# Attention in a two-layer hybrid trunk: row maximum negated, and exponentials issued, per pair of heads

## The chip, the cores and the metric

The kernel runs on one core of a Trainium2 chip. The core's engines work side by side, each through its own queue in order, and meet at semaphores: TensorE (PE: matrix products and transposes; PEld is its loading of stationary operands), VectorE (DVE), ScalarE (ACT), GpSimd (POOL), and SyncE (SP), which here only issues DMAs. The metric is the device time of one execution in microseconds; the value shown is a median of runs.

## The reference

Two layers of a decoder trunk over 512 tokens of width 1024 in float32. Each layer normalises x, projects it to 6400 columns, runs two groups of heads side by side (a gated linear recurrence, HGRN2, and sliding-window attention with a learned sink per head), gates both, projects back and adds. The attention has 16 query heads of 64 and 2 key/value heads. The part that the change touches is the softmax with sink over a window of 128 keys:

```python
def sliding_window_attention(q, k, v, sinks):
    ...
    s = jnp.einsum('bnqkgd,bnskd->bnkgqs', qb, kw).astype(jnp.float32) * ATT_SCALE
    ...
    band = (diff >= 0) & (diff < WINDOW)
    ...
    s = jnp.where(mask[None, :, None, None, :, :], s, NEG_INF)
    sink = jnp.broadcast_to(sinks.astype(jnp.float32).reshape(KV, G)[None, None, :, :, None, None],
                            s.shape[:-1] + (1,))
    p = jax.nn.softmax(jnp.concatenate([s, sink], axis=-1), axis=-1)[..., :-1]
    o = jnp.einsum('bnkgqs,bnskd->bnqkgd', p.astype(v.dtype), vw)

def hybrid_layer(x, w_in, w_out, g_pre, g_post, lb, g_head, sinks):
    h = rms_norm(x, g_pre)
    proj = jnp.einsum('bsd,de->bse', h, w_in)
    ...
    y = jnp.einsum('bse,ed->bsd', jnp.concatenate([o_h, o_a], axis=-1), w_out)
    return x + rms_norm(y, g_post)
```

## The kernel before

**Projections.** Float32 products are made of three products each: every operand is split into a rounded part and a rest (`hi`, `lo`), and `mm3` (L174 to L177) issues lo x hi, hi x lo and hi x hi. Weights come in pieces of 128x512 (`raw`, a DMA on SP), ACT casts each (`whi`, L169) and DVE, for one slab POOL, subtracts (`wlo`, L170); nine pairs of buffers hold them. A slab is eight pieces, 512 columns of the projection. `step()` issues one `mm3` and keeps loading and casting a few pieces ahead.

**Attention.** Layer by layer, `run()` (L769) merges the attention stream with the projection steps of the following slabs (inputs and forget gates): of two streams, the one that is least far on comes next. So PE always has projection products between the attention's small ones. The stream goes through 16 units (g, n): g is a group of four heads, n a block of 128 queries. At its i-th turn it issues `att_scores` of unit i, `att_transpose` of unit i-2 and `att_value` of unit i-4.

- `att_scores` (L406): PE computes the scores of four heads. For n = 0 (units 0, 4, 8, 12) there is one block of keys, and four heads fit one bank of PSUM: DVE masks (copy_predicated L420) and takes the max (L421). For the other twelve units each head has two blocks of keys, so two banks are used, two heads in each, which I call the first and the second half: on each half DVE puts the valid score of the two blocks in one place (copy_predicated L432, by the mask of the window) and takes the max (L433). Then, for all four heads, DVE makes `negm` (the smaller of the negated scaled max and the negated sink, L436) and `ds` (sink plus negm, L438), and ACT makes four exponentials from PSUM to `s` with their row sums (L442) and the exponential of `ds` (L445). DVE adds and inverts the sums (L446, L447), and POOL multiplies `s` with the result (L449).
- `att_transpose` (L452): four transposes on PE into a bank (L455), which ACT casts (`a`, L267) and DVE subtracts (`lo`, named `a` too, L268); for n > 0 POOL then selects the parts that belong to the current and the previous block of keys (`pcur` or `b`, and `pprev`, L467).
- `att_value` (L474): products with v on PE (L481), a copy on ACT (`u`, L483), an addition on DVE (`oa`, L487).

**Banks.** Three PSUM banks, `sc_78` to `sc_80` in the trace's longer names, go round among the halves of scores and the transposes (and later the recurrence). A new use waits for the last reader of the use before: for scores these are the exponentials, for transposes the `lo` subtraction.

**What sets the order.** The program's order is a wish; a scheduler sets each engine's queue from it by a model of times. Matrix products wrapped in `pin` (`tc.keep_in_program_order`) keep their order among each other. The operations on DVE, ACT and POOL are free to move where their data allow.

Of the kernel before, what the change touches and what calls it, by code (L numbers as in the profile page):

```python
# [10 lines left out]
F32 = mybir.dt.float32  # L11
# [54 lines left out]
def hybrid_kernel(ctx: ExitStack, tc: tile.TileContext, x, wkv, win, wout, g_pre, g_post, lbp, ghead, sinks,  # L66
# [28 lines left out]
    def tmp(tag, dt=F32, n=1):  # L95

        t = tp.tile([P, n, 512] if n > 1 else [P, 512], dt, tag=tag, name=tag, bufs=TB[tag])
        return t
# [225 lines left out]
    def layer(l, last):  # L324
# [81 lines left out]
        def att_scores(g, n):  # L406
            v = g // 2
            q = qs[g]
            hs = slice(4 * g, 4 * g + 4)
            t_ = slice(n * P, (n + 1) * P)  # L410
            mx_ = sm.tile([P, 4], F32, tag="mx", name="mx")
            cur = []
            if n == 0:
                S = sc()
                for h in range(4):
                    for p in range(2):
                        pin(nc.tensor.matmul(S[:, h * P:(h + 1) * P], lhsT=q[:, h, t_], rhs=kst[v][p][:, 0:P],
                                         start=(h == 0 and p == 0), stop=(h == 3 and p == 1)))
                Sv = S.rearrange("p (h s) -> p h s", h=4)
                nc.vector.copy_predicated(Sv, am4, neg.unsqueeze(2).broadcast_to([P, 4, P]))  # L420
                nc.vector.tensor_reduce(mx_, Sv, axis=AX.X, op=ALU.max)  # L421
                cur = [Sv[:, h, :] for h in range(4)]
            else:
                for hp_ in range(2):
                    S = sc()
                    for h in range(2):
                        for p in range(2):
                            pin(nc.tensor.matmul(S[:, h * 256:(h + 1) * 256], lhsT=q[:, 2 * hp_ + h, t_],  # L428
                                             rhs=kst[v][p][:, (n - 1) * P:(n + 1) * P],
                                             start=(h == 0 and p == 0), stop=(h == 1 and p == 1)))  # L430
                    Sv = S.rearrange("p (h s) -> p h s", h=2)
                    nc.vector.copy_predicated(Sv[:, :, P:2 * P], am2, Sv[:, :, 0:P])  # L432
                    nc.vector.tensor_reduce(mx_[:, 2 * hp_:2 * hp_ + 2], Sv[:, :, P:2 * P], axis=AX.X, op=ALU.max)  # L433
                    cur += [Sv[:, h, P:2 * P] for h in range(2)]
            negm = sm.tile([P, 4], F32, tag="negm", name="negm")
            nc.vector.scalar_tensor_tensor(negm, mx_, -SCALE, nsnk[:, l, hs], op0=ALU.mult, op1=ALU.min)  # L436
            ds_ = sm.tile([P, 4], F32, tag="ds", name="ds")
            nc.vector.tensor_tensor(ds_, snk[:, l, hs], negm, op=ALU.add)  # L438
            pt = tmp("s")
            sums = sm.tile([P, 4], F32, tag="sums", name="sums")  # L440
            for h in range(4):
                nc.scalar.activation(pt[:, h * P:(h + 1) * P], cur[h], AF.Exp, bias=negm[:, h:h + 1], scale=SCALE,  # L442
                                     accum_out=sums[:, h:h + 1])
            es = sm.tile([P, 4], F32, tag="es", name="es")
            nc.scalar.activation(es, ds_, AF.Exp)  # L445
            nc.vector.tensor_tensor(sums, sums, es, op=ALU.add)  # L446
            nc.vector.reciprocal(sums, sums)  # L447
            pv = pt.rearrange("p (h s) -> p h s", h=4)
            nc.gpsimd.tensor_tensor(pv, pv, sums.unsqueeze(2).broadcast_to([P, 4, P]), op=ALU.mult)  # L449
            return pt  # L450
# [458 lines left out]
```

## Time and profile before

| | us |
|---|---|
| median of three runs | 962.07 (960.97 to 962.83) |
| the profiled execution, its own time | 959.31 |
| its span, first to last instruction | 957.6 |
| PE busy in the span | 921.2 (96%) |
| DVE busy | 683.7 (71%) |
| ACT busy | 478.4 (50%) |
| POOL busy | 268.9 (28%) |
| mean granted clock of PE | 0.986 |
| attention of layer 0, of layer 1 | about 79 to 186, 551 to 658 from the span's start |

The engines overlap, so busy times don't add up to the span. A wait counts for the time only where PE waits, or where something waits for it that PE waits for. In a timeline a row is one instruction or several of a kind in a row, with its start, its time, and in brackets the idle time of the engine ahead of it and what ended that by the profile. The granted clock is that of PE as a share of full speed.

### The profile page before, as it was taken

The page shows a single profiled execution, that of the slowest core. Times are in us where ns is not written, and L with a number is a line of the kernel's source. Part 1 is how long each engine was busy: PE and PEld are TensorE (multiplying, and loading weights), DVE is VectorE, ACT ScalarE, POOL GpSimd, SP SyncE. Part 2 cuts the span into 40 slices and gives each one's busy share as a digit, 9 for nine tenths or more (in the row PEclk, how much of TensorE's full clock was granted, in tenths as well). Part 3 has the DMA queues.
Part 4 walks back from the last instruction along what each step waited for, and adds up shares of the span by engine and source line. Part 5 has one row for each costly group of instructions (what it writes and reads, how often), then busy time and mean ns, then how long its engine had stood idle before and what let it go on. Part 6 is the DMA issues. An engine that isn't in the chain of part 4 may idle for free.

```text
span 957.6 us, 19092 instructions
## 1 busy us (share of the span) xinstructions
PE 921.2 (96%) x7228; PEld 757.5 (79%) x7228; DVE 683.7 (71%) x1382; ACT 478.4 (50%) x1135; POOL 268.9 (28%) x282
## 2 busy tenths in 40 slices
PE   7999999999999999999979998999999999999996
PEld 5888777777878888788868886877788887887885
DVE  5766888786757785765794678878867568849546
ACT  5434656836545462334552365676374545514242
POOL 2322454422231221211231234434322213113102
PEclk9999999999999999999989999999999999999998
DMA  6366433122413343324452775112223123513313
GB/s 227 101 197 201 137 81 89 52 71 67 122 46 89 90 132 89 107 71 112 133 163 66 198 209 155 34 56 88 79 58 98 55 79 100 155 51 107 88 45 132
DMA packets 56716, 101.34 MB, mean 106 GB/s; under 512 B 6448, under 2 KB 8880, under 8 KB 56624
## 3 DMA queue, kind: packets, MB, share of 16 engines
q1 hardware_dynamic: 56624, 100.12, 35.1%
q8 instruction: 57, 0.93, 0.4%
q14 instruction: 35, 0.29, 0.1%
HBM read 87.52 MB, written 12.58 MB: 105 GB/s over the span
## 4 chain that ended last, share of the span: by engine, by line
PE 78%; DVE 11%; ACT 6%; issue 2%; POOL 2%; DMA 1%; SPq 0%; DVEq 0%; POOLq 0%; ACTq 0%
PE pj L175 22%; PE pj L177 22%; PE pj L176 21%; DVE wlo L170 3%; PE sc L583 2%; PE sc L428 2%; PE ac L652 1%; ACT s L442 1%; PE ac L655 1%; PE ac L640 1%; DVE oa L487 1%; PE ac L481 1%; DVE q L600 1%; PE sc L455 1%; PE sc L700 1%
## 5 line engine op out<-in xcount | busy, mean ns | idle before, releaser
L169 ACT CAST whi<-raw 128x512 fp32r<-128x512 f32 x256 | 157.2, 621 | 131.2 <-PE pj L177 61.0
L170 DVE TENSOR_TENSOR wlo<-raw,whi 128x512 fp32r<-128x512 f32 x248 | 190.1, 778 | 44.8 <-ACT whi L169 42.4
L175 PE MATMUL pj<-hhi,wlo 128*128 128x512 f32 x512 | 206.0, 402 | 0.0
L177 PE MATMUL pj<-hhi,whi 128*128 128x512 f32 x512 | 200.1, 391 | 0.0
L176 PE MATMUL pj<-hlo,whi 128*128 128x512 f32 x512 | 199.5, 390 | 0.0
L177 PEld LDWEIGHTS pj<-hhi,whi 128*128 128x128 f32 x512 | 96.1, 188 | 21.0
L175 PEld LDWEIGHTS pj<-hhi,wlo 128*128 128x128 f32 x512 | 96.2, 188 | 18.6
L176 PEld LDWEIGHTS pj<-hlo,whi 128*128 128x128 f32 x512 | 96.3, 188 | 18.0
L175 PE MATMUL pj<-whi,ops 128*128 128x512 f32 x256 | 103.8, 406 | 0.0
L175 PE MATMUL pj<-whi,hlo 128*128 128x512 f32 x256 | 103.0, 405 | 0.0
L176 PE MATMUL pj<-wlo,hhi 128*128 128x512 f32 x256 | 102.1, 399 | 0.0
L177 PE MATMUL pj<-whi,hhi 128*128 128x512 f32 x256 | 101.4, 396 | 0.0
L177 PE MATMUL pj<-whi,ops 128*128 128x512 f32 x256 | 100.1, 391 | 0.0
L176 PE MATMUL pj<-wlo,ops 128*128 128x512 f32 x256 | 99.7, 390 | 0.0
L601 POOL TENSOR_TENSOR k<-k,tot 128x256 f32<-128x256 f32 x80 | 66.0, 844 | 109.5 <-PE sc L583 60.5
L600 DVE TENSOR_TENSOR q<-q,tot 128x256 f32<-128x256 f32 x80 | 48.3, 629 | 14.5 <-PE sc L594 7.6
L442 ACT ACTIVATE s<-sc,negm 128x128 f32<-128x128 f32 x128 | 45.6, 370 | 25.7 <-DVE negm L436 25.4
L449 POOL TENSOR_TENSOR s<-s,sums 128x512 f32<-128x512 f32 x32 | 34.4, 1074 | 83.4 <-DVE sums L447 47.9
L177 PEld LDWEIGHTS pj<-whi,hhi 128*128 128x128 f32 x256 | 48.9, 191 | 10.2
L177 PEld LDWEIGHTS pj<-whi,ops 128*128 128x128 f32 x256 | 48.0, 188 | 10.7
L176 PEld LDWEIGHTS pj<-wlo,hhi 128*128 128x128 f32 x256 | 49.2, 192 | 8.4
L175 PEld LDWEIGHTS pj<-whi,hlo 128*128 128x128 f32 x256 | 48.8, 191 | 8.6
(172 smaller groups left out, 1594.8 us busy)
## 6 DMA issues: line engine op xcount, KB each, us to landing
raw<-in_win_dram SPq DMA_DIRECT2D x192, 256.0 KB, 2.7
raw<-in_wout_dram SPq DMA_DIRECT2D x64, 256.0 KB, 2.7
stack<-rot SPq DMA_DIRECT2D x16, 512.0 KB, 4.4
qs<-stack SPq DMA_DIRECT2D x32, 256.0 KB, 5.0
a<-in_x_dram SPq DMA_DIRECT2D x12, 256.0 KB, 2.9
raw<-in_wkv_dram SPq DMA_DIRECT2D x8, 256.0 KB, 4.0
x_mid<-a SPq DMA_DIRECT2D x8, 256.0 KB, 2.1
a<-x_mid SPq DMA_DIRECT2D x8, 256.0 KB, 2.9
```

Source lines behind the costliest of these rows:

```text
L169: nc.scalar.copy(hi, v)
L170: (nc.gpsimd if i in on_pool and i % 2 else nc.vector).tensor_tensor(lo, v, hi.bitcast(F32), op=ALU.subtract)
L175: nc.tensor.matmul(o, lhsT=sta[1], rhs=mov[0], start=start, stop=False)
L176: nc.tensor.matmul(o, lhsT=sta[0], rhs=mov[1], start=False, stop=False)
L177: nc.tensor.matmul(o, lhsT=sta[0], rhs=mov[0], start=False, stop=stop)
L428: pin(nc.tensor.matmul(S[:, h * 256:(h + 1) * 256], lhsT=q[:, 2 * hp_ + h, t_], rhs=kst[v][p][:, (n - 1) * P:(n + 1) * P], start=(h == 0 a ...
L442: nc.scalar.activation(pt[:, h * P:(h + 1) * P], cur[h], AF.Exp, bias=negm[:, h:h + 1], scale=SCALE, accum_out=sums[:, h:h + 1])
L449: nc.gpsimd.tensor_tensor(pv, pv, sums.unsqueeze(2).broadcast_to([P, 4, P]), op=ALU.mult)
L455: pin(nc.tensor.transpose(T[:, h * P:(h + 1) * P], pt[:, h * P:(h + 1) * P], ident))
L583: pin(nc.tensor.matmul(L[32 * b:32 * b + 32, c:c + 16], lhsT=k[:, o_:o_ + 32], rhs=qv[:, blk:blk + qu, 1, :], start=True, stop=True, tile_ ...
L600: nc.vector.tensor_tensor(qv[:, :, 1, :], qv[:, :, 1, :], tv[:, :, 0].unsqueeze(2).broadcast_to([P, nb, hh]), op=ALU.mult)
L601: nc.gpsimd.tensor_tensor(kv_[:, :, 0, :], kv_[:, :, 0, :], tv[:, :, 1].unsqueeze(2).broadcast_to([P, nb, hh]), op=ALU.mult)
```

## The change

In `att_scores` the buffers are taken at the top, and a helper `exps` makes negm for the heads it is given, two columns or four, and at once their exponentials. It is called after each half's max, no longer once after both. `pin` on the second half's copy_predicated keeps the order of such operations among pinned ones on DVE. `ds` and all that follows stay for four heads at a time. There are 24 more negm operations, 12 in each layer; no other operation is added or taken away. The lines of the changed kernel differ: negm is L417, the exponentials L420, copy_predicated L430 and L442, max L431 and L445, `ds` L447, `es` L449, sums L450 and L451, the multiply L453; from there on each line is 4 higher.

```diff
@@ -408,8 +408,18 @@
             q = qs[g]
             hs = slice(4 * g, 4 * g + 4)
             t_ = slice(n * P, (n + 1) * P)
-            mx_ = sm.tile([P, 4], F32, tag="mx", name="mx")
-            cur = []
+            mx_, negm, ds_, sums = (sm.tile([P, 4], F32, tag=n_, name=n_) for n_ in ("mx", "negm", "ds", "sums"))
+            pt = tmp("s")
+
+            def exps(first, cur):
+
+                c = slice(first, first + len(cur))
+                nc.vector.scalar_tensor_tensor(negm[:, c], mx_[:, c], -SCALE, nsnk[:, l, 4 * g + first:4 * g + first + len(cur)],
+                                               op0=ALU.mult, op1=ALU.min)
+                for h, src in enumerate(cur, first):
+                    nc.scalar.activation(pt[:, h * P:(h + 1) * P], src, AF.Exp, bias=negm[:, h:h + 1], scale=SCALE,
+                                         accum_out=sums[:, h:h + 1])
+
             if n == 0:
                 S = sc()
                 for h in range(4):
@@ -419,7 +429,7 @@
                 Sv = S.rearrange("p (h s) -> p h s", h=4)
                 nc.vector.copy_predicated(Sv, am4, neg.unsqueeze(2).broadcast_to([P, 4, P]))
                 nc.vector.tensor_reduce(mx_, Sv, axis=AX.X, op=ALU.max)
-                cur = [Sv[:, h, :] for h in range(4)]
+                exps(0, [Sv[:, h, :] for h in range(4)])
             else:
                 for hp_ in range(2):
                     S = sc()
@@ -429,18 +439,12 @@
                                              rhs=kst[v][p][:, (n - 1) * P:(n + 1) * P],
                                              start=(h == 0 and p == 0), stop=(h == 1 and p == 1)))
                     Sv = S.rearrange("p (h s) -> p h s", h=2)
-                    nc.vector.copy_predicated(Sv[:, :, P:2 * P], am2, Sv[:, :, 0:P])
+                    cp = nc.vector.copy_predicated(Sv[:, :, P:2 * P], am2, Sv[:, :, 0:P])
+                    if hp_:
+                        pin(cp)
                     nc.vector.tensor_reduce(mx_[:, 2 * hp_:2 * hp_ + 2], Sv[:, :, P:2 * P], axis=AX.X, op=ALU.max)
-                    cur += [Sv[:, h, P:2 * P] for h in range(2)]
-            negm = sm.tile([P, 4], F32, tag="negm", name="negm")
-            nc.vector.scalar_tensor_tensor(negm, mx_, -SCALE, nsnk[:, l, hs], op0=ALU.mult, op1=ALU.min)
-            ds_ = sm.tile([P, 4], F32, tag="ds", name="ds")
+                    exps(2 * hp_, [Sv[:, h, P:2 * P] for h in range(2)])
             nc.vector.tensor_tensor(ds_, snk[:, l, hs], negm, op=ALU.add)
-            pt = tmp("s")
-            sums = sm.tile([P, 4], F32, tag="sums", name="sums")
-            for h in range(4):
-                nc.scalar.activation(pt[:, h * P:(h + 1) * P], cur[h], AF.Exp, bias=negm[:, h:h + 1], scale=SCALE,
-                                     accum_out=sums[:, h:h + 1])
             es = sm.tile([P, 4], F32, tag="es", name="es")
             nc.scalar.activation(es, ds_, AF.Exp)
             nc.vector.tensor_tensor(sums, sums, es, op=ALU.add)
```

The scheduler makes another order of it on all engines, within the attention stages only, and the same in both layers. Three places follow, all in layer 0: unit 7 on DVE and on ACT, units 2 to 5 on PE, and the stage's start on POOL.

On DVE, from unit 7's first half on, before:

```order
L432 COPY_PREDICATED sc_78<-masks,sc_78 128x2x128
L446 TENSOR_TENSOR sums<-sums,es 128x4
L433 TENSOR_REDUCE mx<-sc_78 128x2
L447 RECIPROCAL sums<-sums 128x4
L432 COPY_PREDICATED sc_79<-masks,sc_79 128x2x128
L268 TENSOR_TENSOR a<-sc_80,a 128x512
L170 TENSOR_TENSOR wlo<-raw,whi 128x512 x3
L433 TENSOR_REDUCE mx<-sc_79 128x2
L487 TENSOR_TENSOR oa<-ac,u 64x2x128
L436 SCALAR_TENSOR_TENSOR negm<-mx,nsnk 128x4
L487 TENSOR_TENSOR oa<-ac,u 64x2x128
L438 TENSOR_TENSOR ds<-snk,negm 128x4
```

The same place in the changed kernel:

```order
L442 COPY_PREDICATED sc_78<-masks,sc_78 128x2x128
L445 TENSOR_REDUCE mx<-sc_78 128x2
L450 TENSOR_TENSOR sums<-sums,es 128x4
L417 SCALAR_TENSOR_TENSOR negm<-mx,nsnk 128x2
L451 RECIPROCAL sums<-sums 128x4
L170 TENSOR_TENSOR wlo<-raw,whi 128x512
L442 COPY_PREDICATED sc_79<-masks,sc_79 128x2x128
L170 TENSOR_TENSOR wlo<-raw,whi 128x512
L445 TENSOR_REDUCE mx<-sc_79 128x2
L417 SCALAR_TENSOR_TENSOR negm<-mx,nsnk 128x2
L447 TENSOR_TENSOR ds<-snk,negm 128x4
L268 TENSOR_TENSOR a<-sc_80,a 128x512
```

Unit 7's first max is now followed by a negm of two columns, ahead of the weight subtractions (`wlo`) that lay between the first copy and the second half's max; one `wlo` stands between the two halves' small steps, and two others have moved.

On ACT around unit 7's exponentials, before:

```order
L169 CAST whi<-raw 128x512 x2
L483 COPY u<-ac 64x512
L169 CAST whi<-raw 128x512
L442 ACTIVATE s,sums<-sc_78,negm 128x128 x2
L442 ACTIVATE s,sums<-sc_79,negm 128x128 x2
L445 ACTIVATE es<-ds 128x4
```

In the changed kernel (exponentials L420):

```order
L420 ACTIVATE s,sums<-sc_78,negm 128x128
L169 CAST whi<-raw 128x512
L420 ACTIVATE s,sums<-sc_78,negm 128x128
L516 COPY vt<-pj 128x512
L267 CAST a<-sc_80 128x512
L420 ACTIVATE s,sums<-sc_79,negm 128x128 x2
L449 ACTIVATE es<-ds 128x4
```

The two halves' exponentials stand further apart, with a weight cast, a copy and a cast of transposes between them.

On PE, from the transposes of unit 2 (the first row's `sc_80`) to those of unit 3, before:

```order
L455 MATMUL sc_80<-ident,s 128x128 x4
L481 MATMUL ac<-pcur,vst 128x512 x2
L481 MATMUL ac<-pprev,vst 128x512 x2
L175 MATMUL pj<-whi,hlo 128x512
L176 MATMUL pj<-wlo,hhi 128x512
L177 MATMUL pj<-whi,hhi 128x512
L175 MATMUL pj<-whi,hlo 128x512
L455 MATMUL sc_80<-ident,s 128x128 x4
```

In the changed kernel, where the transposes of unit 2 stand two rows ahead of this piece, and the row between is one product L177:

```order
L438 MATMUL sc_78<-kst,qs 128x256 x4
L176 MATMUL pj<-wlo,hhi 128x512
L177 MATMUL pj<-whi,hhi 128x512
L175 MATMUL pj<-whi,hlo 128x512
L176 MATMUL pj<-wlo,hhi 128x512
L177 MATMUL pj<-whi,hhi 128x512
L485 MATMUL ac<-pcur,vst 128x512 x2
L485 MATMUL ac<-pprev,vst 128x512 x2
L175 MATMUL pj<-whi,hlo 128x512
L176 MATMUL pj<-wlo,hhi 128x512
L459 MATMUL sc_80<-ident,s 128x128 x4
```

The first half of unit 5's scores (into `sc_78`) has moved behind the transposes of unit 2, and more products stand between the transposes of unit 2 and of unit 3, whose bank is the same.

On POOL, the first operations of the attention stage, before (L449 is the multiply of a unit's exponentials, L467 the two selections):

```order
L449 TENSOR_TENSOR s<-s,sums 128x512 x3
L467 AFFINE_SELECT pcur<-a 128x1024
L467 AFFINE_SELECT pprev<-a 128x1024
L449 TENSOR_TENSOR s<-s,sums 128x512
L467 AFFINE_SELECT b<-a 128x1024
L467 AFFINE_SELECT pprev<-a 128x1024
L449 TENSOR_TENSOR s<-s,sums 128x512
L467 AFFINE_SELECT pcur<-a 128x1024
```

In the changed kernel, where these are L453 and L471:

```order
L453 TENSOR_TENSOR s<-s,sums 128x512 x4
L471 AFFINE_SELECT pcur<-a 128x1024
L471 AFFINE_SELECT pprev<-a 128x1024
L471 AFFINE_SELECT b<-a 128x1024
L471 AFFINE_SELECT pprev<-a 128x1024
L471 AFFINE_SELECT pcur<-a 128x1024
L453 TENSOR_TENSOR s<-s,sums 128x512
L471 AFFINE_SELECT pprev<-a 128x1024
```

Four multiplies now stand ahead of the first selections, and a selection of unit 3 ahead of the multiply of unit 4.

## Rows read from the trace of the kernel before

**Rows 1.** The page's first part: busy time, share of the span, instructions

```profile
PE 921.2 (96%) x7228; PEld 757.5 (79%) x7228; DVE 683.7 (71%) x1382; ACT 478.4 (50%) x1135; POOL 268.9 (28%) x282
```

**Rows 2.** Windows: stretch, length, busy us of five engines, PEclk, DMA share, GB/s

```profile
78.00:190.00 112.00, 105.26 (x529) 86.24 (x529) 88.07 (x199) 74.22 (x226) 49.23 (x43) 0.97 0.36 104
550.00:662.00 112.00, 105.08 (x535) 86.00 (x534) 89.42 (x199) 75.82 (x228) 49.32 (x44) 0.98 0.38 106
200.00:312.00 112.00, 110.76 (x1220) 90.79 (x1220) 77.77 (x145) 58.14 (x116) 30.58 (x36) 1.00 0.27 77
100.00:110.00 10.00, 7.84 (x37) 6.31 (x36) 8.36 (x20) 4.78 (x17) 6.02 (x7) 0.83 0.63 179
110.00:120.00 10.00, 10.00 (x56) 8.18 (x55) 7.77 (x24) 7.32 (x26) 2.74 (x3) 1.00 0.20 55
120.00:130.00 10.00, 8.27 (x38) 6.88 (x37) 8.32 (x16) 4.82 (x15) 4.59 (x5) 0.83 0.70 183
570.00:580.00 10.00, 7.71 (x43) 5.93 (x42) 9.68 (x20) 7.34 (x26) 6.15 (x6) 1.00 0.87 234
590.00:610.00 20.00, 18.27 (x91) 15.16 (x90) 17.10 (x40) 10.82 (x39) 11.45 (x10) 0.91 0.41 107
```

**Rows 3.** Waits of PE: line <- releaser: us in total, times, longest

```profile
PE sc L455 <- DVE negm L436: 3.9, 2, 2.0
PE sc L417 <- ACT s L442: 3.5, 2, 1.7
PE sc L428 <- ACT s L442: 3.3, 4, 1.3
PE sc L455 <- ACT s L442: 0.4, 2, 0.2
```

**Rows 4.** Timeline of PE, layer 0: start, us, instructions [idle before]

```profile
105.33 0.84 PE L455 MATMUL sc<-ident,s 128*128 128x128 f32 x4 [1.96 <-DVE negm L436]
125.44 1.40 PE L417 MATMUL sc<-kst,qs 128*128 128x128 f32 x8 [1.73 <-ACT s L442]
161.51 1.43 PE L428 MATMUL sc<-kst,qs 128*128 128x256 f32 x8 [1.27 <-ACT s L442]
185.06 0.73 PE L481 MATMUL ac<-pcur,vst 128*128 128x512 f32 x2 [0.56 <-POOL pcur L467]
```

**Rows 5.** Timeline of DVE ahead of the stall at 105.33

```profile
104.50 0.68 DVE L268 TENSOR_TENSOR a<-sc,a 128x512 fp32r<-128x512 f32 x1
```

**Rows 6.** Timeline of DVE ahead of the stall at 125.44

```profile
118.55 0.42 DVE L433 TENSOR_REDUCE mx<-sc 128x2 f32<-128x256 f32 x1
119.89 3.92 DVE L170 TENSOR_TENSOR wlo<-raw,whi 128x512 fp32r<-128x512 f32 x3
123.73 0.41 DVE L433 TENSOR_REDUCE mx<-sc 128x2 f32<-128x256 f32 x1
124.40 0.14 DVE L436 SCALAR_TENSOR_TENSOR negm<-mx,nsnk 128x4 f32<-128x4 f32 x1
```

**Rows 7.** Timeline of ACT over the same stretch

```profile
124.57 0.37 ACT L442 ACTIVATE s<-sc,negm 128x128 f32<-128x128 f32 x1 [3.24 <-DVE negm L436]
```

**Rows 8.** Groups of instructions by form: busy us, mean ns | idle before

```profile
L267 ACT CAST a<-sc 128x512 fp32r<-128x512 f32 x32 | 18.9, 590 | 15.9 <-PE sc L455 14.5 <-POOL s L449 1.0
L436 DVE SCALAR_TENSOR_TENSOR negm<-mx,nsnk 128x4 f32<-128x4 f32 x32 | 7.2, 225 | 0.6
```

**Rows 9.** Timeline of DVE at 133.9: one negm

```profile
133.93 0.82 DVE L436 SCALAR_TENSOR_TENSOR negm<-mx,nsnk 128x4 f32<-128x4 f32 x1
```

**Rows 10.** Timeline of POOL beside it

```profile
133.64 1.09 POOL L467 TENSOR_SCALAR_AFFINE_SELECT pcur<-a 128x1024 fp32r<-128x1024 f32 x1 [0.34 <-DVE a L268]
```

**Rows 11.** Timeline of POOL: one unit's multiply and its two selections

```profile
96.75 1.04 POOL L449 TENSOR_TENSOR s<-s,sums 128x512 f32<-128x512 f32 x1 [6.15 <-PE ac L481]
98.03 1.10 POOL L467 TENSOR_SCALAR_AFFINE_SELECT pcur<-a 128x1024 fp32r<-128x1024 f32 x1 [0.24 <-DVE negm L436]
99.08 1.54 POOL L467 TENSOR_SCALAR_AFFINE_SELECT pprev<-a 128x1024 fp32r<-128x1024 f32 x1
```

## The prediction

> **What bounds the kernel now.** I read the busy times first. TensorE (PE) is busy 96% of the span [rows 1]; no other engine comes near, so only PE's gaps can be won. The windows by stage say where gaps lie. In the stretch after layer 0's attention PE is busy 110.76 of 112 us, but in the two attention stages it is busy 105.26 and 105.08 of 112 [rows 2]: 6.7 and 6.9 us idle, in stages where DVE (88 and 89 us) and POOL (49) still have room on average. The table of PE's waits names what ended last [rows 3]: transposes behind DVE (3.9 us), scores of units with n = 0 behind exponentials (3.5), scores of other units behind exponentials (3.3), transposes behind exponentials (0.4): 11.1 us together. The timeline shows three places per layer, in layer 0 at 105.33 (1.96 us), 125.44 (1.73) and 161.51 (1.27) [rows 4]; I call them A, B and C. In layer 1 the counts and longest waits repeat them.
>
> A carries a second name in the profile. It is put down to negm, but the order of PE shows that the transposes of unit 3 reuse the bank of unit 2's, so they need its `lo` subtraction, which ran from 104.50 to 105.18 [rows 5], late in a full DVE queue. B is plain: the max of unit 7's first half began at 118.55, its negm only at 124.40, because the second half's max stood behind three weight subtractions of 3.92 us together [rows 6]; ACT waited 3.24 us for that [rows 7], and unit 8's scores waited for the bank that the first half's exponentials read. C is the same pattern at unit 13.
>
> The clock is the second price. The granted clock is 0.83 in the windows of A and B of layer 0, and 0.91 over 20 us at B of layer 1, against 1.00 elsewhere; at A of layer 1 it stays 1.00 [rows 2]. The two levels are 1.2 and 2.4 GHz, so 10 x 0.17 + 10 x 0.17 + 20 x 0.09 = 5.2 us of PE's work were lost. In each of the three PE had just stood idle for about 1.7 to 2 us. So 11.1 + 5.2 = 16.3 us is all that the change can take away.
>
> **The change, part by part.** *Removed: B.* Negm and two exponentials follow directly on the first half's max, ahead of the weight subtractions. By the rows of before the first half's negm would be done near 119.1 instead of 124.5 [rows 6]; two exponentials of 0.37 [rows 7], and the one weight cast that ACT now puts between them (0.6), end by some 121, and unit 8's scores would like to begin at 125.44 - 1.73 = 123.7 [rows 4]. There are over 2 us of slack, so B goes whole: 3.5 us in both layers, and 1.7 + 1.8 us of clock.
>
> *Moved: A.* The transposes of units 2 and 3 stand further apart in PE's new order (16 instructions of projection, scores and values between, against 8), so unit 2's `lo` has more cover. A's 1.96 us and its 1.7 us of clock go; what comes instead is listed below.
>
> *Shortened: C.* Unit 13's first half no longer waits for its second, but its own second half does what both did before, and part of the wait stays.
>
> *Added: 24 negm operations*, one for each of 12 units per layer. By the group one takes 0.225 us in the mean; alone 0.14 [rows 6, 8]. So 24 x 0.14 = 3.4 to 24 x 0.82 = 19.7 us of DVE (the upper end by the slow negm below); I take the mean, 5.4 us, or 2.7 a layer. DVE is idle 112 - 88 = 24 us in that stage [rows 2]: that hides it, except where DVE stands full, as ahead of A. The pinned order costs overlap between DVE's neighbours; I cost it at nothing for the same reason, up to A again.
>
> A small operation beside POOL is the price to watch. A negm began at 133.93 and took 0.82 us while POOL's selection ran from 133.64 to 134.73 [rows 9, 10]; alone it takes 0.14 [rows 6]. The Trainium skill, "SBUF — State Buffer", section "SBUF: two separate sides", has a rule that speaks against this change: VectorE with two SBUF inputs and GpSimd take a shared port in turn, each for its whole instruction, so that the other is blocked. Negm has two such inputs (mx and nsnk), and the row agrees with the rule. By it every added negm that falls into POOL's busy share, 49 of 112 us, would wait out on average half a selection, 24 x 0.44 x 0.55 = 5.8 us (an estimate); if all of that reached PE, the sum below would be -3.4 and the time 958.7. By the rows DVE's idle time takes it, except at the places listed next.
>
> *New or remaining waits of PE.* I followed the new order by hand from the rows; each place is bounded by nothing below (PE arrives later than the data) and above by the nearest row. Per layer:
> - transposes of unit 2 behind the second exponentials of unit 3: 0 to 0.7 (two exponentials); taken 0.35, nearer to the 0.2 that a transpose waits for exponentials now [rows 3].
> - first scores of unit 5 behind unit 1's `lo`: between those transposes and the scores PE has 17 instructions, at 10.00 / 56 = 0.18 each [rows 2] 3.1 us of cover; needed are the cast (0.59 [rows 8]) and `lo` (0.68 [rows 5]), and ahead of them a weight subtraction (3.92 / 3 = 1.3 [rows 6]) and the two small steps of the sums: 3.0 to 3.9. Range 0 to 1.96 (A, the same kind of wait), taken 0.75.
> - value product of unit 1 behind its second selection: POOL now does four multiplies before the first selections. Range 0 to 1.04, one multiply [rows 11]; taken 0.35, nearer to the 0.56 that a value product waits for POOL at the end of the stage [rows 4].
> - transposes of unit 4 behind its multiply, which POOL now begins after unit 3's first selection: 0 to 1.10 + 1.04 = 2.14 [rows 11]; taken 0.85.
> - second scores of unit 6 behind unit 5's second exponentials: 0 to 1.27 (C, the same wait [rows 4]); taken 0.45.
> - C's rest: 0 to 1.27; taken 0.8, since its second negm stands behind a POOL selection.
>
> Sum 3.55 per layer, 7.1 in all; the upper ends give 8.4 per layer, 16.8. None of the six is taken as long as the idle stretches ahead of the three clock drops, and C's 1.27 brought none: the stage's mean clock of 0.97 over 112 us, 3.4 us, is used up by the windows of A and B [rows 2].
>
> *Queues passed.* On SP four loads of the query tile go out three weight loads earlier than before, once per layer. They have a transfer's room (DMA share 0.63 and 0.70 in the windows of A and B [rows 2]), and casts stand several weights ahead of PE: nothing, unless a weight comes late, which PE's waits of before never show in these stages.
>
> **Sum.** 959.31 us is the profiled run; -16.3 + 7.1 = -9.2 gives 950.1. That run lies 2.8 us under the median of 962.07, so by the median's scale 952.9, call it 953. After the stage PE is busy almost throughout, so nothing gives the shift back; nor does anything add to it.
>
> **Rivals.**
> 1. *The new waits are all hidden*: every lower end holds, -16.3, 945.8. For it: DVE's mean idle time. Against: DVE is full where A stood (9.68 of 10 us in layer 1's window [rows 2]).
> 2. *The waits only change place*: the six at their upper ends, -16.3 + 16.8, 962.6. For it: banks, DVE and POOL are close to each other in units 1 to 5. Against: all six would have to be at their ends at once.
> 3. *Slower: POOL blocks the second negm.* In the twelve units with two halves the second negm, and so the exponentials, the scores in the next bank and the multiply that POOL itself waits for, come 0.82 - 0.14 = 0.68 us later, and the added operation takes up to 0.82 before it as well; if DVE has no idle time at these places, 1.5 us per unit reach PE: 24 x 1.5 = 36, less 16.3, +19.7, about 982. It decides from 16.3 / 24 = 0.68 us per unit on, that is when nearly half of it reaches PE. Against it: DVE's 24 idle us; a middle case (1 us per unit) gives 970.
> 4. *The change does not do what it says*: the scheduler sets ACT's order, and in the new one casts stand between the exponentials of one half. If those come late enough, unit 8's bank stays taken and B stays with its clock: -16.3 + 7.0 + 7.1 = -2.2, about 960. Against: the 2 us of slack above.
>
> **How the numbers follow.** My forecast, a part of the gain (948 to 958), has 0.54; rival 1 0.13; rival 2 0.12, rival 3 0.13, rival 4 0.08. A measurement of this kernel tells about 0.2% (1.9 us) from no change. Faster: 0.54 + 0.13 + half of rival 4 (0.04) + a quarter of rival 2 (0.03) = 0.74. Slower: 0.13 + a quarter of rival 2 (0.03) = 0.16. The same: 0.10. The range from 945 to 965 leaves out most of rival 3 and a little below rival 1, under 0.2. The likeliest case's own range is 948 to 958.
>
> **What would show it.** Right: in the attention stages PE's idle time falls from 13.6 us to about 7; no wait of scores with n = 0 behind exponentials; no granted clock under 0.95 in any 10 us there; ACT's 3.24 us wait for negm ahead of B gone. Step A wrong: a transpose or the first scores of unit 5 wait over 1.7 us and the clock falls in layer 0 again. Rival 3: negm above 0.5 us in the mean of its group, and transposes waiting for POOL's multiply. What would make it all wrong is a wait of PE that stands in none of the six places.

## The result, and the profile after

The changed kernel takes 965.18 us (median of 7 runs, 962.75 to 968.43) against 961.36 for the kernel before (median of 7, 960.75 to 962.83): ratio 1.0046, 95% interval 1.0032 to 1.0061. It is slower by about 4 us; forecast was 9 us faster.

The profiled run of after took 968.43 us, the longest of its seven, with a span of 966.7. A part of that is not the change's: the first scores of layer 0, which stand behind work that both kernels share, began at 79.18 before and at 83.41 after. So I compare the attention stages, not the spans. First the windows of the stages of after, each as long as that of [rows 2] and shifted with the work; then some windows of ten microseconds, those of layer 0 under full clock among them (columns as in [rows 2]):

```profile
82.00:194.00 112.00, 103.71 (x514) 84.45 (x514) 88.38 (x205) 72.94 (x222) 49.34 (x43) 0.95 0.37 103
557.00:669.00 112.00, 102.72 (x528) 83.25 (x527) 90.78 (x208) 74.52 (x225) 49.51 (x43) 1.00 0.38 107
130.00:140.00 10.00, 7.94 (x33) 5.62 (x32) 9.16 (x17) 4.23 (x14) 6.03 (x6) 0.93 0.10 26
140.00:150.00 10.00, 10.00 (x47) 8.58 (x46) 5.27 (x15) 4.98 (x15) 1.04 (x1) 0.73 0.17 56
160.00:170.00 10.00, 8.06 (x41) 6.31 (x40) 9.74 (x20) 5.93 (x20) 5.22 (x6) 0.96 0.33 100
170.00:180.00 10.00, 10.00 (x47) 8.32 (x47) 5.94 (x19) 8.59 (x22) 2.07 (x2) 0.87 0.00 0
610.00:620.00 10.00, 7.94 (x39) 5.77 (x38) 7.43 (x17) 5.25 (x17) 3.49 (x3) 1.00 0.26 79
```

PE's idle time is 8.3 and 9.3 us where it was 6.7 and 6.9 [rows 2]: 3.9 us more. The granted clock took as much as before in sum: by the windows shown 10 x (0.07 + 0.27 + 0.04 + 0.13) = 5.1 us in layer 0 and nothing in layer 1, against 5.2 us before [rows 2]. So idle time makes the 4 us. The mean clock of all runs says the same: the median is 0.987 for the changed kernel (7 runs) and 0.986 for the kernel before (21 later runs). PE's waits in the whole run, those of the attention stages:

```profile
PE sc L438 <- ACT s L420: 4.3, 7, 1.4
PE pj L176 <- DVE wlo L170: 3.0, 4, 1.0
PE sc L459 <- POOL s L453: 2.3, 2, 1.2
PE ac L485 <- POOL pprev L471: 1.8, 3, 0.8
PE ac L485 <- POOL pcur L471: 1.8, 2, 1.3
PE ac L485 <- DVE oa L491: 1.3, 1, 1.3
PE pj L175 <- ACT whi L169: 1.1, 2, 0.6
PE sc L438 <- DVE a L268: 0.8, 2, 0.4
```

The rows of [rows 3] on transposes behind DVE and on scores with n = 0 are gone: A and B did go. New are two rows of projection products (`pj`) that wait for weights, 4.1 us together. The timeline of PE in layer 0 gives each its place (columns as in [rows 4]):

```profile
104.26 0.74 PE L438 MATMUL sc<-kst,qs 128*128 128x256 f32 x4 [0.40 <-DVE a L268]
107.39 0.73 PE L485 MATMUL ac<-pprev,vst 128*128 128x512 f32 x2 [0.77 <-POOL pprev L471]
113.39 0.44 PE L459 MATMUL sc<-ident,s 128*128 128x128 f32 x2 [1.16 <-POOL s L453]
115.62 0.74 PE L438 MATMUL sc<-kst,qs 128*128 128x256 f32 x4 [0.41 <-ACT s L420]
135.77 0.73 PE L175 MATMUL pj<-whi,hlo 128*128 128x512 f32 x2 [0.56 <-ACT whi L169]
137.72 0.50 PE L176 MATMUL pj<-wlo,hhi 128*128 128x512 f32 x1 [0.98 <-DVE wlo L170]
139.21 0.79 PE L176 MATMUL pj<-wlo,hhi 128*128 128x512 f32 x1 [0.51 <-DVE wlo L170]
168.49 0.74 PE L438 MATMUL sc<-kst,qs 128*128 128x256 f32 x4 [1.37 <-ACT s L420]
```

The first four are waits of the prediction's list. The next three, 2.05 us, stand in none of its places; layer 1 has the same three at 611 to 615. The last is C.

Where the weights were shows on SP, the timeline of its DMA issues. Before:

```profile
102.75 15.15 SPq L152 DMA_DIRECT2D raw<-in_win_dram  x3
118.72 1.75 SPq L397 DMA_DIRECT2D qs<-stack  x4
```

The second and third of these loads, before:

```profile
116.59 1.31 SPq L152 DMA_DIRECT2D raw<-in_win_dram  x2
```

After:

```profile
119.88 1.75 SPq L397 DMA_DIRECT2D qs<-stack  x4
121.73 18.39 SPq L152 DMA_DIRECT2D raw<-in_win_dram  x6
```

Before, three weight loads (the 35th to the 37th) were issued at 102.75, 116.59 and 117.58, and then the four fetches of the query tile of group 3. These fetches need the buffer that unit 7's scores read last; those end at 118.69 before and at 119.85 after, so the fetches can't start earlier. In the changed kernel they stand ahead of those three loads, which therefore wait until 121.73, 122.21 and 122.71. With the run's later start of 4.2 us taken off, the first load is 15 us later than before, and the other two about 1 us. The time from the issue of these three to their landing, in the changed kernel:

```profile
DMA to landing us min/median/max: 5.7/5.9/6.1
```

So all three had landed by 128.8. After, timelines of ACT, DVE and POOL where these weights are used:

```profile
132.50 0.37 ACT L420 ACTIVATE s<-sc,negm 128x128 f32<-128x128 f32 x1 [2.74 <-DVE negm L417]
...
135.10 1.66 ACT L169 CAST whi<-raw 128x512 fp32r<-128x512 f32 x3
```

```profile
134.62 1.06 DVE L450 TENSOR_TENSOR sums<-sums,es 128x4 f32<-128x4 f32 x1
...
136.66 3.10 DVE L170 TENSOR_TENSOR wlo<-raw,whi 128x512 fp32r<-128x512 f32 x3
```

```profile
136.08 1.04 POOL L453 TENSOR_TENSOR s<-s,sums 128x512 f32<-128x512 f32 x1 [0.40 <-DVE sums L451]
137.07 1.55 POOL L471 TENSOR_SCALAR_AFFINE_SELECT pprev<-a 128x1024 fp32r<-128x1024 f32 x1
```

The three casts begin without a wait of their own, over 6 us after the last of their weights had landed. So it is not the transfer that holds them but their place on ACT: they stand behind unit 9's exponentials, for whose negm ACT had waited 2.74 us. Before, they ran at 118.80, 119.32 and 120.71, ahead of unit 7's exponentials, the second and third of them within 0.3 us of the landing of their weights. The three subtractions then take 3.10 us while POOL multiplies and selects.

### The profile page after: what moved, and what is told of

Same layout as the page of the kernel before. It is cut to its first block, busy times and chain, and to the rows that moved or that the text cites. A ratio compares the mean times of both kernels' runs of the same rounds, so it can differ in the third digit from the quotient of the medians.

```text
span 966.7 us, 19140 instructions
## 1 busy us (share of the span) xinstructions
PE 923.3 (96%) x7228; PEld 758.1 (78%) x7228; DVE 689.4 (71%) x1406; ACT 479.0 (50%) x1135; POOL 269.2 (28%) x282
## 4 chain that ended last, share of the span: by engine, by line
PE 73%; DVE 15%; ACT 5%; issue 3%; POOL 2%; DMA 1%; SPq 0%; DVEq 0%; POOLq 0%; ACTq 0%
PE pj L175 21%; PE pj L177 21%; PE pj L176 21%; DVE wlo L170 3%; ACT s L420 2%; PE sc L587 2%; PE ac L656 1%; DVE negm L417 1%; PE sc L438 1%; DVE oa L491 1%; PE ac L659 1%; PE ac L644 1%; DVE q L604 1%; DVE xn L306 1%; DVE mx L445 1%
## 5 line engine op out<-in xcount | busy, mean ns | idle before, releaser
L170 DVE TENSOR_TENSOR wlo<-raw,whi 128x512 fp32r<-128x512 f32 x248 | 185.9, 761 | 44.9 <-ACT whi L169 42.6
L177 PE MATMUL pj<-hhi,whi 128*128 128x512 f32 x512 | 200.8, 392 | 0.0
L177 PEld LDWEIGHTS pj<-hhi,whi 128*128 128x128 f32 x512 | 96.7, 189 | 21.3
L177 PE MATMUL pj<-whi,hhi 128*128 128x512 f32 x256 | 101.8, 397 | 0.0
L177 PE MATMUL pj<-whi,ops 128*128 128x512 f32 x256 | 100.1, 391 | 0.0
L420 ACT ACTIVATE s<-sc,negm 128x128 f32<-128x128 f32 x128 | 46.0, 368 | 42.7 <-DVE negm L417 36.3
L453 POOL TENSOR_TENSOR s<-s,sums 128x512 f32<-128x512 f32 x32 | 34.9, 1092 | 83.4 <-ACT a L267 44.4
L177 PEld LDWEIGHTS pj<-whi,ops 128*128 128x128 f32 x256 | 48.0, 188 | 10.7
L177 PEld LDWEIGHTS pj<-whi,hhi 128*128 128x128 f32 x256 | 48.7, 190 | 9.7
```

The costliest lines, as they stand in the source:

```text
L170: (nc.gpsimd if i in on_pool and i % 2 else nc.vector).tensor_tensor(lo, v, hi.bitcast(F32), op=ALU.subtract)
L177: nc.tensor.matmul(o, lhsT=sta[0], rhs=mov[0], start=False, stop=stop)
L420: nc.scalar.activation(pt[:, h * P:(h + 1) * P], src, AF.Exp, bias=negm[:, h:h + 1], scale=SCALE, accum_out=sums[:, h:h + 1])
```

## The experiments

Two readings stood against each other. Theory W: the loss is the weight supply, through SP's order. Theory N: the loss is the 24 added operations and the finer order on DVE and POOL.

### One part undone, one part alone

The fetch of group 3's query tile moved into the attention stream, in the changed kernel:

```diff
-                st = big.tile([P, 4, 512], F32R, tag="b8", name="qs", bufs=2)
-                for row, j, i in ((0, 1, 0), (32, 0, 1), (64, 0, 0), (96, 1, 1)):
-                    nc.sync.dma_start(st[row:row + 32].bitcast(F32), stack[j, i].rearrange("(h p) t -> p h t", h=4))
-                qs[g] = st
+                def fetch():
+                    st = big.tile([P, 4, 512], F32R, tag="b8", name="qs", bufs=2)
...
+                    qs[g] = st
+
+                if g == 3:
+                    qs[g] = None
+                    fetch_3.append(fetch)
+                else:
+                    fetch()
...
             for i in range(n + VLAG):
+                if i == 8:
+                    fetch_3.pop()()
```

> The changed kernel, but the query tile of group 3 is fetched from inside the attention stream (turn 8) instead of ahead of it; everything else is the changed kernel's text. In SP's queue two more weight loads then stand ahead of the first of the four fetches (stack, r2, Q1, r3, Q1, r1, Q2 in place of stack, Q4, r62). Theory W (the loss is the weight supply: loads queued on SP behind the fetches, which wait for unit 7's scores to free their buffer): the three waits of projection products for whi and wlo (0.56, 0.98, 0.51 us in the changed kernel's layer 0, the same in layer 1) and the 6.8 us at half clock that followed in layer 0 are gone; 2.05 x 2 + 3.4 = 7.5 us less than the changed kernel where its clock fell, 4.1 where not: about 958 to 961, ratio to before 0.997 to 1.000. Theory N (the loss is the added negm operations and the finer order, blocked by POOL and DVE): the waits of scores, transposes and values stay, no change against the changed kernel: 964 to 966, ratio 1.003 to 1.005.

Measured: 960.34 us, ratio 0.9996 (0.9982 to 1.0011). The loss is gone and the waits for weights with it, as W said. The small waits of units 2 to 6 stay to the hundredth (0.40, 0.77, 1.16, 0.41), so they are not what made the kernel slower than before; they eat a part of what A and B gave. C's wait for exponentials is 2.31 us in this run, more than in the changed kernel.

The changed kernel without the pin:

```diff
-                    if hp_:
-                        pin(cp)
```

> The changed kernel without the pin on the second half's copy_predicated: negm and exponentials per pair of heads alone. SP's queue then has the order of the kernel before (three weight loads ahead of the last four fetches), with all 24 added negm operations kept. Theory W: no wait of projection products for weights, so at or under the kernel before: 957 to 962, ratio 0.996 to 1.000. Theory N: the added operations cost what they cost in the changed kernel: 963 to 966, ratio 1.002 to 1.005.

Measured: 960.03 us, ratio 0.9993 (0.9979 to 1.0008). All added operations are there and nothing is lost: N falls. SP's order is that of before, and no product waits for weights. Stall A has stayed, with 2.1 us.

The kernel before with the pin alone:

```diff
-                    nc.vector.copy_predicated(Sv[:, :, P:2 * P], am2, Sv[:, :, 0:P])
+                    cp = nc.vector.copy_predicated(Sv[:, :, P:2 * P], am2, Sv[:, :, 0:P])
+                    if hp_:
+                        pin(cp)
```

> The kernel before with the pin alone: copy_predicated of second halves kept in program order, negm and exponentials for four heads at once as before. SP's queue has the last four fetches behind six weight loads, so weights are not late. Theory W: no wait of projection products for weights; stall B (scores of n = 0 behind exponentials, 1.73 us per layer) stays, since the negm still waits for the second half: 960 to 964, ratio 0.999 to 1.002. Theory N: without added operations no loss: 959 to 962. The two theories do not part here; the run tells what the pin alone moves.

Measured: 959.38 us, ratio 0.9990 (0.9978 to 1.0002). No difference that can be told; B is smaller (0.70 us), A too (1.54), and other waits came in their place.

The kernel before with SP's order of the changed kernel, made with pins on the fetches of group 3 and on the 35th weight load:

```diff
+    behind_qs = {slab_first["in", l, IV + 1][0] + 6 for l in range(DEPTH)}
...
-            nc.sync.dma_start(t.rearrange("p (a c) -> p a c", a=2) if len(src.shape) == 3 else t, src)
+            load = nc.sync.dma_start(t.rearrange("p (a c) -> p a c", a=2) if len(src.shape) == 3 else t, src)
+            if i in behind_qs:
+                pin(load)
...
-                    nc.sync.dma_start(st[row:row + 32].bitcast(F32), stack[j, i].rearrange("(h p) t -> p h t", h=4))
+                    load = nc.sync.dma_start(st[row:row + 32].bitcast(F32), stack[j, i].rearrange("(h p) t -> p h t", h=4))
+                    if g == 3:
+                        pin(load)
```

> The kernel before, with the four fetches of group 3's query tile kept ahead of the 35th weight load on SP, as the scheduler set them in the changed kernel (SP's queue is the changed kernel's, row by row). No operation is added and none of the score steps is changed. Theory W: the weights come late here too, waits of projection products of about 2 us per layer behind whi and wlo appear between units 8 and 11, with or without half a clock window: 4 to 8 us more than before: 965 to 969, ratio 1.004 to 1.008. Theory N: nothing of what costs is here: 960 to 963, ratio 0.999 to 1.002.

Measured: 955.88 us, ratio 0.9949 (0.9932 to 0.9967): faster, where W said slower by 4 to 8 us. So W falls too in its simple form. PE, DVE and POOL at the same place in this run:

```profile
137.73 0.97 PE L178 MATMUL pj<-whi,hlo 128*128 128x512 f32 x3 [0.56 <-ACT whi L172]
```

```profile
138.07 1.90 DVE L173 TENSOR_TENSOR wlo<-raw,whi 128x512 fp32r<-128x512 f32 x3
```

```profile
135.20 1.04 POOL L454 TENSOR_TENSOR s<-s,sums 128x512 f32<-128x512 f32 x1 [0.40 <-DVE sums L452]
```

The loads stand behind the fetches as in the changed kernel, and the casts run as late, at 137.06, 7 us after the landing: PE waits 0.56 us for `whi`, the same. But POOL had finished at 136.24, the three subtractions take 1.90 us and not 3.10, and no product waits for `wlo`. And B is gone without any split: the subtractions that stood between the two halves of unit 7 are no longer there.

### The three parts together

I formed a new theory, I: late weights, that is late casts and subtractions, take the subtractions out of B's place, which is a gain; they cost only where POOL works beside the subtractions. Two more runs fill the table, with the edits above put together.

> Negm and exponentials per pair of heads, no pin, and the four fetches of group 3's query tile kept ahead of the 35th weight load on SP (as in the changed kernel). With the runs so far it fills the table of the three parts: split alone 960.0, pin alone 959.4, fetches first alone 955.9, split and pin with fetches late 960.3, all three (the changed kernel) 965.2. Theory I (the late weights are harmless by themselves and even take weight subtractions out of stall B's place; they cost only where DVE, beside POOL's multiply and selection, is too slow for the three subtractions): it depends on what POOL does at that place; as the order of the exponentials is the split one, I expect a wait for wlo of 0.5 to 1.5 us per layer and 958 to 963, ratio 0.997 to 1.002. Theory S (the split order cannot stand late weights at all): like the changed kernel, 963 to 967, ratio 1.002 to 1.006. Theory P (it is the pinned order on DVE that cannot stand them): like the fetches first alone, 955 to 957, ratio 0.993 to 0.996.

Measured: 958.02 us, ratio 0.9964 (0.9951 to 0.9977), with no wait of products for weights above 0.15 us. The wait for `wlo` that I gave for theory I is a miss, and the ratio lies at the lower edge of its range; S falls, and P's range (0.993 to 0.996) is just missed.

> The pin alone, with negm and exponentials for four heads at once as before, and the four fetches kept ahead of the 35th weight load on SP. Theory I: as for the split, by the place of POOL's operations; stall B gone as in the run with the fetches first alone, 954 to 960, ratio 0.993 to 0.999. Theory S: without the split late weights cost 0.56 us per layer, 955 to 958. Theory P: waits for whi and wlo of about 2 us per layer, 961 to 966.

Measured: 960.09 us, ratio 0.9986 (0.9975 to 0.9997), with 0.57 us for `whi` and 0.36 for `wlo`, the latter not at the late weights but earlier, at 122.8. P falls. B is smaller but not gone, as I had expected it to be: scores of unit 8 wait 0.48 us in layer 0 and 0.77 in layer 1.

| split of negm | pin | fetches ahead of the loads | ratio to before | 95% |
|---|---|---|---|---|
| - | - | - | 1 | |
| x | - | - | 0.9993 | 0.9979 to 1.0008 |
| - | x | - (*) | 0.9990 | 0.9978 to 1.0002 |
| x | x | - (*) | 0.9996 | 0.9982 to 1.0011 |
| - | - | x | 0.9949 | 0.9932 to 0.9967 |
| x | - | x | 0.9964 | 0.9951 to 0.9977 |
| - | x | x | 0.9986 | 0.9975 to 0.9997 |
| x | x | x (the changed kernel) | 1.0046 | 1.0032 to 1.0061 |

(*) The order on SP is near that of before but not the same. Only the three together lose. The worth of the fetches' place goes from -0.5% to +0.5% by what the order on DVE and POOL makes of it.

Weights one piece further ahead, LEAD = 5 in the changed kernel:

```diff
-LEAD = 4
+LEAD = 5
```

> The changed kernel with LEAD = 5 in place of 4: weights are cast and their loads issued one piece further ahead of PE throughout. SP's queue still has one weight load or more behind the last four fetches. All theories of the weight supply: the waits for whi and wlo between units 8 and 11 fall under 0.6 us per layer and the time to 957 to 962, ratio 0.996 to 1.001. Theory N (added operations and finer order): 964 to 966.

Measured: 966.92 us, ratio 1.0059 (1.0036 to 1.0082). A miss: the waits for weights fell only from 2.05 to 1.26 us in layer 0, and the stage got a new stall at its start, where scores wait 3.65 us for exponentials (3.25 in layer 1). All orders differ in this run, so it says little on the changed kernel:

```profile
89.46 0.74 PE L438 MATMUL sc<-kst,qs 128*128 128x256 f32 x4 [3.65 <-ACT s L420]
```

### POOL taken away from the late subtractions

The changed kernel without unit 7's second selection and unit 9's multiply, in each layer; the queues of DVE, ACT and SP stay the same:

```diff
+                if which == 1 and (g, n) == (1, 3):
+                    terms += [(n - which, d[:, 0]), (n - which, d[:, 1])]
+                    continue
...
-            nc.gpsimd.tensor_tensor(pv, pv, sums.unsqueeze(2).broadcast_to([P, 4, P]), op=ALU.mult)
+            if (g, n) != (2, 1):
+                nc.gpsimd.tensor_tensor(pv, pv, sums.unsqueeze(2).broadcast_to([P, 4, P]), op=ALU.mult)
```

> The changed kernel with two POOL operations per layer left out where the late weight subtractions run: unit 7's second selection (its previous block is read from the current block's tile) and unit 9's multiply. The attention of units 7 and 9 is then not the reference's; DVE, ACT and SP keep the changed kernel's queues row by row, PE keeps its order. Theory I (the late weights cost because three subtractions take 3.1 us beside POOL in place of 1.9): the three subtractions take 1.9 to 2.1 us, the waits of projection products for wlo fall from 1.49 to 0 to 0.5 us per layer, the wait for whi (0.56) stays, and the half clock after them goes: 962 to 963.5 where the changed kernel's clock fell there, ratio 0.998 to 1.002 to before. Theory L (the casts alone are too late, whatever POOL does): the waits stay near 2 us per layer, 964 to 966, ratio 1.002 to 1.005.

Measured: 963.38 us, ratio 1.0017 (1.0006 to 1.0028). DVE and PE at the place:

```profile
134.70 1.07 DVE L450 TENSOR_TENSOR sums<-sums,es 128x4 f32<-128x4 f32 x1
...
136.74 1.90 DVE L170 TENSOR_TENSOR wlo<-raw,whi 128x512 fp32r<-128x512 f32 x3
```

```profile
135.84 0.73 PE L175 MATMUL pj<-whi,hlo 128*128 128x512 f32 x2 [0.52 <-ACT whi L169]
137.49 0.50 PE L176 MATMUL pj<-wlo,hhi 128*128 128x512 f32 x1 [0.68 <-DVE wlo L170]
```

The subtractions take 1.90 us, as I said; the waits for `wlo` fall from 1.49 to 0.68, a little more than the 0.5 I gave. The small operation on the sums still takes 1.07 beside the first selection of unit 7, and holds the subtractions back.

With that selection left out as well:

```diff
+            if (g, n) == (1, 3):
+                return [(n, tt_[:, 0]), (n, tt_[:, 1]), (n - 1, tt_[:, 0]), (n - 1, tt_[:, 1])]
```

> As the run before it, and unit 7's first selection left out too (its values read the cast transposes directly), so that the small sums operation ahead of the subtractions is not slowed either. Up to the three subtractions the queues of DVE, ACT and SP are the changed kernel's; behind them they differ. Theory I: sums 0.16 us in place of 1.06, the three subtractions start about 0.9 us earlier and take 1.9 us, no wait for wlo. Theory L: waits of 1 us and more for wlo stay.

```profile
130.46 0.16 DVE L450 TENSOR_TENSOR sums<-sums,es 128x4 f32<-128x4 f32 x1
...
131.94 1.90 DVE L170 TENSOR_TENSOR wlo<-raw,whi 128x512 fp32r<-128x512 f32 x3
```

No product waits for `wlo` in either layer, and `whi` still costs 0.51 and 0.55. That is theory I: of the 2.05 us, 1.49 is POOL's doing and 0.56 that of the late casts. The one time, 954.77 us, is not to be set beside the others, since the queues differ behind this place.

### Two tiles early

The kernel before with the fetches of the last two groups ahead of the 31st and the 35th load (`j in (2, 6)`, `if g >= 2`):

> The kernel before with the fetches of the last two query tiles kept ahead of the 31st and the 35th weight load on SP. Unit 3's and unit 7's places on DVE then hold fewer weight subtractions. Theory I: what the fetches first did for stall B (from 1.73 us to 0) they do in part for stall A (1.96 us): 952 to 956, ratio 0.991 to 0.995. Against it: late weights are waited for, 0.56 us more per layer at a second place, or stall A does not come from the subtractions: 955 to 960, ratio 0.994 to 0.999.

Measured: 955.27 us, ratio 0.9945 (0.9930 to 0.9960), the same as with one tile within the intervals. The time is in theory I's range, but not for the reason that I gave: stall A went from 1.96 only to 1.81, though two of the three subtractions ahead of it were gone (one of 1.47 us stayed). In the profiled run neither attention stage had a window under full clock. Both this and the run with one tile are faster than the two kernels of this case.

> As the run before it, with negm and exponentials per pair of heads (no pin). Theory I: the split gains little once the subtractions are out of the way, 953 to 958, ratio 0.992 to 0.997; if the split has a worth of its own, under the run before it.

Measured: 958.14 us, ratio 0.9971 (0.9960 to 0.9983), just above the range. Products wait for `wlo` again, 0.27 and 1.18 us in layer 0. With the fetches placed so, the split costs about 2.5 us (0.9971 against 0.9945); it has no worth of its own here.

## Why the prediction was wrong

**What held.** The bound (PE's gaps in two stages) and the removal of A and B: no scores with n = 0 wait for exponentials in the changed kernel, and unit 8's scores began at 123.79, before their time of [rows 4], though the run had started 4.2 us later. A went only with the split and the pin together: it is 2.10 us without the pin and 1.54 with the pin alone. The five small waits of units 2 to 6 came where they were put, none other among them; the first is too small to tell, since the profile names no releaser for its 0.16 us:

| wait, layer 0 | taken | measured |
|---|---|---|
| transposes of unit 2 | 0.35 | 0.16 |
| first scores of unit 5, `lo` | 0.75 | 0.40 |
| values of unit 1, selection | 0.35 | 0.77 |
| transposes of unit 4, multiply | 0.85 | 1.16 |
| second scores of unit 6 | 0.45 | 0.41 |
| C's rest | 0.8 | 1.94 (0.39 + 0.18 + 1.37) |

Five of them make 2.90 us against 2.75 taken.

**The step that failed** is "Queues passed". It cost the four fetches that go ahead of three weight loads at nothing, with a transfer's room and casts "several weights ahead of PE" as the cover. The room was there: the loads landed by 128.8. The price was order. The fetches wait for a buffer until unit 7's scores are through, the loads stand behind them, and on ACT the three casts went from ahead of unit 7's exponentials to behind unit 9's, where POOL then slowed their subtractions. So the casts no longer stood ahead of PE. The step named the case itself ("unless a weight comes late") and dismissed it because the trace of before had no such wait; there the loads were ahead. Measured: 2.05 us in each layer, 4.1 us of the 13 between forecast and result. The excerpts of ACT's order showed it as well: the three casts that stood ahead of unit 7's exponentials are missing in the changed kernel's (the one cast there is an earlier one), and I did not ask where they had gone. It is also the last of the prediction's own signs: a wait of PE that stands in none of the six places.

The fetches' place and the casts' place go together in the other runs too. In the four kernels of the table with the loads ahead of the fetches, or mostly so (its first four rows), the second and third of these casts start within 0.3 us of the landing of their weights. In the eight kernels with all four fetches ahead of the 35th load and LEAD = 4, the changed kernel among them, the three casts start 4.8 to 8.2 us after it. That the scheduler moves the casts because of the fetches fits this, but its reasons are not in the traces.

**The clock** was to give back 5.2 us and gave nothing: 5.2 us before and 5.1 after, by the windows of ten microseconds. The three stalls ahead of its falls were gone, but new ones took their place in layer 0. Behind the 2.05 us at the weights the clock is 0.93 and 0.73, 3.4 us; that is the same failed step, priced once more. Behind C's waits it is 0.96 and 0.87, 1.7 us, where the prediction had counted on C bringing none.

**C** was mis-sized: 1.94 us a layer for 0.8 and outside its range of 0 to 1.27, 2.3 us in both. It was read as what the second negm leaves; in the new order unit 13's and 14's scores wait three times, and longer than before (0.36 + 1.27 = 1.63). Without the pin, and with the fetches ahead, three waits at that place come to 1.0 us (0.34 + 0.38 + 0.26). The stage's end was not in the sum: values wait 1.25 us in layer 0 and 1.25 + 0.53 + 0.29 in layer 1, some 1 us more than before in sum.

So idle time: 13.6 before, 9.6 forecast, 17.6 measured; of the 8.0 between, 4.1 are the weights, 2.3 C and about 1 the end; the rest is in small waits. With the 5.1 us of clock that did not come back this makes 13.1, about the 13 between forecast and result; 4.1 + 3.4 = 7.5 of it stand at and behind the weights. (The sign "about 7" us of idle time did not follow from the prediction's own sum, which gives 13.6 - 11.1 + 7.1 = 9.6.)

**The rivals.** The time went past rival 2 (the waits change place, 0.5 us slower than before) to 3.8 us slower, though five of its six waits stayed below their upper ends; C's rest went over its 1.27, and a wait outside the six places did the most. Rival 3 had the right pair, POOL against DVE operations, but mostly at the wrong ones: negm took 0.306 us in the mean of 48, and the run without the pin shows that the added ones cost nothing that can be told.

```profile
L417 DVE SCALAR_TENSOR_TENSOR negm<-mx,nsnk 128x2 f32<-128x2 f32 x48 | 14.7, 306 | 1.1
```

One slow negm does stand in the path: that of unit 9's first half, beside a selection of POOL, ahead of the exponentials that hold up the late casts. What its 0.94 us cost there was not measured.

```profile
131.47 0.94 DVE L417 SCALAR_TENSOR_TENSOR negm<-mx,nsnk 128x2 f32<-128x2 f32 x1
```

```profile
131.30 1.09 POOL L471 TENSOR_SCALAR_AFFINE_SELECT pprev<-a 128x1024 fp32r<-128x1024 f32 x1
```

What POOL slowed to the price of time were the weight subtractions, also operations with two operands in SBUF. The Trainium skill, "SBUF — State Buffer", section "SBUF: two separate sides", which says that such an operation and a GpSimd instruction that reads SBUF shut each other out, is borne out by the two runs with POOL's operations left out: 1.90 us for three subtractions without POOL, 3.10 beside it.

**What stays open.** Why the pin, the split and the early fetches each are harmless and only together put POOL's multiply on the subtractions is the scheduler's doing; the runs show that it is so. No run kept the fetches ahead and put only the casts back. At C neither part alone makes the loss: the waits there are 1.66 us with the pin alone, 1.34 with the split alone and 1.94 with both (2.49 with the late fetch), against 1.63 before; why both together cost more is open.

## What to carry to other kernels

An instruction that a scheduler moves ahead on an in-order queue is not priced by its own length: ask when its buffer comes free, what then stands behind it, and where the work that hangs on that now stands on the other engines. Where an excerpt of an order shows work that has left a place, follow it to where it went before the gain is counted. And before splitting an operation to shorten a wait, look at what stands between its halves: here moving the foreign work away (one line's order on the DMA queue) took the same stall out, for a gain of 0.5% instead of a loss.

## What the runs showed of the hardware

Three 128x512 subtractions with both operands in SBUF took 1.90 us with POOL idle and 3.10 beside its multiply and selection; an addition of 128x4 took 0.16 and 1.06. The clock does not answer a stall each time: behind the waits of 0.56, 0.98 and 0.51 us it was 0.93 and 0.73 in layer 0, and behind the same three of 0.56, 0.97 and 0.53 in layer 1 it stayed 1.00. Behind C it stayed 1.00 before, after 1.27 us, and in the changed kernel fell to 0.87 in layer 0 but not in layer 1, after 1.37 us in both.
